# Two output projections of a hybrid transformer on one core: a place of its own for the second chunk of a weight sum, and evictions and norm weights moved to other units and engines

## The chip, the cores and the metric

The kernel runs on one core of a Trainium2 chip. The metric is the device time in microseconds (us) of one execution. One execution was also taken with the hardware profiler, which records every instruction of TensorE (PE, with its weight loads PEld), VectorE (DVE), ScalarE (ACT), GpSimd (POOL) and SyncE (SP), and the DMA transfers.

## The reference, cut to what matters

A model of two layers on 512 tokens of width 1024, all in float32. Layer 0 is attention followed by a gated feed-forward block, layer 1 is an mLSTM followed by another, and a final norm ends it. The change sits in the second half of the two feed-forward blocks and in the final norm:

```
def swiglu(xn, w_in, w_out):
    gu = xn @ w_in
    return (jax.nn.silu(gu[..., :D_FF]) * gu[..., D_FF:]) @ w_out
...
        h = h + swiglu(rms_norm(h, ffn_norm[i]), ffn_w_in[i], ffn_w_out[i])
    return rms_norm(h, final_norm)
```

D_FF is 2816. The product with w_out (2816 by 1024) is called the output projection here; the first one belongs to layer 0, the last one to layer 1. The final norm divides each token's 1024 values by the root of their mean square and multiplies by final_norm, the norm weights.

## The kernel before, in words

**Precision.** Each float32 operand is split into a high part (ACT copies it, rounded) and a low part (DVE subtracts the high part from the original). A product is three matrix products: high by high, low by high, high by low. For a weight chunk the two instructions are lines 209 (ACT) and 210 (DVE) in split_chunk, on 128x1024 values; for an operand of the output projection they are line 1114 (ACT) and the DVE subtraction that is recorded at line 1108.

**The output projection** (output_products, from line 1086). The hidden width is cut into 11 pieces of 256 rows. The first six pieces, paired as three units u = 0, 1, 2, go through a Strassen-like scheme with seven products P1, P2, P5, P6, P7, P3, P4 instead of eight, each made once for every unit; the last five pieces (called rest: 6 to 10) are multiplied plainly, once for each half n of the weight columns. The list items sets the order: P1 three times; P5 and P2 in turn; P6 then P7, in turn with the rest of one half; P3 three times; P4 in turn with the rest of the other half; then the last pieces (tail: 2 in the first projection, 3 in the last). In the last projection the end of that list is P3 u=0, P3 u=1, P3 u=2, P4 u=0, piece 6, P4 u=1, piece 7, P4 u=2, and then pieces 8, 9, 10 as the tail.

work() walks through this list. Ahead of item i it calls prepare for item i+2, which issues the weight loads on SP, the sums of chunks on DVE, and the splits on ACT and DVE. After the last unit of a product it calls the function that then holds for that product: evictions of the accumulators. The tile scheduler puts the instructions of each engine in their final order by dependences and by the order of these calls.

**Places.** Weight chunks of 128x1024 land in a rotating set of three places (tag wraw, line 200); their high and low parts have three places each (whi, wlo). load_chunk (line 198) takes the next wraw place and issues the load on SP at line 201. SP issues its loads in order, so a load that waits for a place holds up those behind it. The tile tag t1 is one place of 128x1024 in the pool of a feed-forward block; in the first half of the block it holds the sums S of Strassen chunks (line 989), and in layer 1 it holds the norm weights gbc afterwards (line 1614).

**P5 in the first projection** (line 1136) needs the sum of two weight chunks. Both are loaded with load_chunk, so each P5 takes two of the three wraw places. DVE adds them at line 1136, subtracts at line 1108 to update the chunk T (places w8), and splits.

**The end of the last projection** (from line 1635). Accumulators are in PSUM banks c11, u_, p5, c22. add_banks (line 1652) adds u_ to the residual tiles ht[tb, 1] on DVE; tb counts the four blocks of 128 tokens, and the second index is the half n of the output columns. output() does, for one accumulator: line 1636, DVE adds it to the residual ht in place; line 1638, ACT squares it and sums the squares into fss; line 1639, GpSimd multiplies ht by the norm weights in place. mean_before (lines 1642 and 1643, DVE) starts the mean. For n = 1 this is done by outputs() after P7 (c22, tb 2 and 3) and after P3 (p5, tb 0 and 1). For n = 0 it is done behind the tail's matmuls, line 1685, tile by tile; the last tile is cut in two halves of 256 columns (finlast is the second). Then lines 1695 to 1700 make the factor r of that block of tokens (DVE, with one square root on ACT), ACT multiplies ht[tb, 1] by r and stores it from its own queue (lines 1702, 1703), and DVE multiplies ht[tb, 0] by r, which SP stores (lines 1704, 1705).

Of the kernel before, what the change touches and what calls it, by code (L numbers as in the profile page):

```python
# [11 lines left out]
F32 = mybir.dt.float32  # L12
F32R = mybir.dt.float32r
I32 = mybir.dt.int32
AF = mybir.ActivationFunctionType
# [56 lines left out]
def tile_hybrid_dilated_attn_mlstm(  # L72
# [1017 lines left out]
    def output_products(layer, fp, wo, sums_of_rows, tail):  # L1090
# [30 lines left out]
        def prepare_product(name, u):  # L1121
            nm = "f%d%s_%dw" % (layer, name, u)
            view = lambda t: t.rearrange("p (k n) -> p k n", k=2)

            def load(hk, n):
                return load_chunk(weight_rows(hk * UNITS + u, n), [P, 2, 512], nm)[0]
            if name == "P1":
                if u % 2 == 0:
                    tw.append(fp.tile([P, 2, 1024], F32, tag="w8", name="f%dT%d" % (layer, u), bufs=2))
                nc.sync.dma_start(view(tw[u // 2][:, u % 2]), weight_rows(u, 0))  # L1130
            t = tw[u // 2][:, u % 2]
            raw = load(*ROWS[name]) if name in ROWS and name != "P1" else t
            if sums_of_rows:

                if name == "P5":
                    nc.vector.tensor_tensor(raw, raw, load(1, 1), op=ALU.add)
                elif name in ("P7", "P3"):
                    subtract(raw, raw, t)
            else:

                if name in ("P5", "P6"):
                    subtract(t, raw, t)
                    raw = t
                elif name == "P7":
                    subtract(raw, t, raw)
                elif name == "P4":
                    subtract(raw, raw, t)
            whl[name, u] = split_chunk((raw, 1024, view, nm))
            if sums_of_rows and name == "P5":
                subtract(t, raw, t)  # L1150

            if name == "P5":
                split_operand(name, u, sums[u])
            elif name == "P6":
                split_operand(name, u, half(u, 1))
            elif name == "P7":
                subtract(sums[u], *((half(u, 1), half(u, 0)) if sums_of_rows else (half(UNITS + u, 1), half(u, 1))))
                split_operand(name, u, sums[u])
            elif name == "P3":
                if not sums_of_rows:  # L1160
                    subtract(half(u, 1), half(UNITS + u, 0), half(u, 1))
                split_operand(name, u, half(UNITS + u, 1) if sums_of_rows else half(u, 1))
            elif name == "P4":
                if sums_of_rows:
                    subtract(half(UNITS + u, 0), half(UNITS + u, 0), half(u, 1))
                split_operand(name, u, half(UNITS + u, 0 if sums_of_rows else 1))
# [51 lines left out]
        def work(product, plain, then):  # L1218

            for i, (kind, *key) in enumerate(items[:-tail]):  # L1220
                prepare(i + AHEAD)
                key = tuple(key)
                if kind == "product":
                    product(*key, ops[key], whl[key])
                    if key[1] == UNITS - 1 and key[0] in then:
                        then[key[0]]()
                else:
                    plain(*key, ops[key[1]], whl[key])
            for i in range(len(items) - tail + AHEAD, len(items)):
                prepare(i)  # L1230
            return [(ops[pi], whl[n, pi]) for _, n, pi in last]
# [3 lines left out]
    with ExitStack() as fctx:  # L1235
        fp = pool(fctx, "ffn0")
        hid, during, prepare, work = output_products(0, fp, ffn_w_out[0], True, 2)
        ffn_in(0, fp, pair, rbc, hook, prepare, hid, during)


        F = [[ps.tile([P, 512], F32, tag=tag, name="fo%d" % n, bufs=3 if tag == "acc" else 2 - (tag == "t"))
              for tag in tags] for n, tags in enumerate((("s", "s", "acc", "acc"), ("o", "o", "acc", "t")))]
        ts = [slice(0, HALF), slice(HALF, SEQ)]
        target = {"P1": (0, 0), "P2": (0, 0), "P5": (0, 1), "P3": (0, 1), "P6": (1, 0), "P7": (1, 0), "P4": (1, 0)}

        def tile_mm(acc, m, b, w, fresh=False):
            for k in range(2):
                for a_, b_ in SPLITS:
                    nc.tensor.matmul(acc, w[a_][:, k, m * P:(m + 1) * P], b[b_][k],  # L1249
                                     start=(fresh and k == 0 and (a_, b_) == SPLITS[0]),  # L1250
                                     stop=(k == 1 and (a_, b_) == SPLITS[-1]), skip_group_check=True)

        def product(name, u, b, w):
            n, t = target[name]
            for m in range(4):
                tile_mm(F[n][m][:, ts[t]], m, b, w, name == "P1" and u == 0)

        def plain(n, pi, b, w):
            for m in range(4):
                tile_mm(F[n][m], m, b, w)  # L1260

        old, h = h, []

        def natural(k, acc):
            t = hp.tile([P, SEQ], F32, tag="h", name="hn%d" % k, bufs=KC + 1)
            nc.vector.tensor_tensor(t.rearrange("p (j c) -> p c j", c=4), acc.rearrange("p (c j) -> p c j", c=4),
                                    old[k].rearrange("p (c j) -> p c j", c=4), op=ALU.add)
            h.append(t)

        def copy_half(t):  # L1270
            for m in range(4):
                nc.scalar.activation(F[1][m][:, ts[t]], F[0][m][:, ts[t]], AF.Copy)

        def add_sum(n):
            for m in range(4):
                o = old[4 * n + m][:, ts[1]]
                nc.vector.tensor_tensor(o, F[1][m][:, ts[0]], o, op=ALU.add)

        def first_tiles():
            for m in range(4):  # L1280
                natural(m, F[0][m])
        last = work(product, plain, {"P1": lambda: copy_half(0), "P5": lambda: copy_half(1),
                                     "P6": lambda: add_sum(0), "P7": lambda: add_sum(1), "P3": first_tiles})
        for m in range(4):
            for b, w in last:
                tile_mm(F[1][m], m, b, w)
            natural(4 + m, F[1][m])
# [298 lines left out]
    with ExitStack() as fctx:  # L1586
# [47 lines left out]
        def output(tb, n, acc, part, cs=slice(0, 512)):  # L1634
            t = ht[tb, n][:, cs]
            nc.vector.tensor_tensor(t, acc[:, cs], t, op=ALU.add)  # L1636
            junk = npl.tile([P, SEQ], F32, tag="sq", name="fsq", bufs=2)
            nc.scalar.activation(junk[:, cs], t, AF.Square, accum_out=fss[:, tb, part:part + 1])  # L1638
            nc.gpsimd.tensor_tensor(t, t, gbc[:, n * 512 + cs.start:n * 512 + cs.stop], op=ALU.mult)

        def mean_before(tb):
            nc.vector.tensor_tensor(fpre[:, tb:tb + 1], fss[:, tb, 0:1], fss[:, tb, 1:2], op=ALU.add)
# [7 lines left out]
        def add_banks(tbs, src):  # L1650
            for m, tb in enumerate(tbs):
                nc.vector.tensor_tensor(ht[tb, 1], src[m], ht[tb, 1], op=ALU.add)
# [13 lines left out]
            for t in range(2):  # L1666
                multiply_half(((c11, u_), (p5, c22))[n][t], a, t, w)

        def after_p7():
            add_banks((2, 3), u_)  # L1670
            outputs((2, 3), c22)
        last = work(product, plain, {"P1": lambda: copy_banks(u_, c11), "P5": lambda: copy_banks(c22, p5),
                                     "P6": lambda: add_banks((0, 1), u_), "P7": after_p7,
                                     "P3": lambda: outputs((0, 1), p5)})

        rest_of = bank("o", "last")
        t = ht[TB - 1, 0][:, 256:]
# [3 lines left out]
        for acc, tb, cs in tiles:  # L1681
# [8 lines left out]
            if cs.stop == 256:  # L1690
                mean_before(tb)
            else:

                v, r, a2 = fv[:, tb:tb + 1], fr[:, tb:tb + 1], fa[:, tb:tb + 1]
                nc.vector.scalar_tensor_tensor(v, fss[:, tb, 2:3], 1.0 / D, fpre[:, tb:tb + 1],  # L1695
                                               op0=ALU.mult, op1=ALU.add)
                nc.scalar.activation(r, v, AF.Sqrt)  # L1697
                nc.vector.reciprocal(r, r)  # L1698
                nc.vector.tensor_scalar(a2, r, v, r, op0=ALU.mult, op1=ALU.mult)  # L1699
                nc.vector.scalar_tensor_tensor(r, a2, -3.0, r, op0=ALU.add, op1=ALU.mult)  # L1700
                t1, t0 = ht[tb, 1], ht[tb, 0]
                nc.scalar.activation(t1, t1, AF.Copy, scale=r)  # L1702
                nc.scalar.dma_start(out[tb * P:(tb + 1) * P, 512:1024], t1)
                nc.vector.tensor_scalar(t0, t0, r, None, op0=ALU.mult)
                nc.sync.dma_start(out[tb * P:(tb + 1) * P, 0:512], t0)


# [22 lines left out]
```

## Time and profile before

| | us |
|---|---|
| median of 3 runs | 1416.81 (1416.67 to 1419.73) |
| the profiled execution | 1416.74 |
| its span, first to last instruction | 1415.0 |
| first projection on PE (line 1249) | 730.9 to 848.4 |
| last projection on PE (lines 1630, 1685) | 1293.6 to 1408.3 |

A row of the timeline gives start, busy time, engine, line, operation and tiles, merged where alike (x2), and in brackets how long the engine was idle before it and whose result ended that. A tile name in the trace leaves out the product's number: f0P_2w_h is the high part of a chunk of unit 2 of some P in the first projection, f1P of the last; f0w and f1w are the rest's chunks, fo and finc, finu, finp, finlast the accumulators. DVE, ACT and PE records overlap a little with the next, because an instruction's record ends after its successor has entered the engine.

### The profile page before, as it was taken

The page shows a single profiled execution, that of the slowest core. Times are in us where ns is not written, and L with a number is a line of the kernel's source. Part 1 is how long each engine was busy: PE and PEld are TensorE (multiplying, and loading weights), DVE is VectorE, ACT ScalarE, POOL GpSimd, SP SyncE. Part 2 cuts the span into 40 slices and gives each one's busy share as a digit, 9 for nine tenths or more (in the row PEclk, how much of TensorE's full clock was granted, in tenths as well). Part 3 has the DMA queues.
Part 4 walks back from the last instruction along what each step waited for, and adds up shares of the span by engine and source line. Part 5 has one row for each costly group of instructions (what it writes and reads, how often), then busy time and mean ns, then how long its engine had stood idle before and what let it go on. Part 6 is the DMA issues. An engine that isn't in the chain of part 4 may idle for free. (4 is left out here: it accounts for less than half of the span.)

```text
span 1415.0 us, 20843 instructions
## 1 busy us (share of the span) xinstructions
PE 1401.2 (99%) x8094; PEld 1235.3 (87%) x8094; DVE 1046.7 (74%) x1798; ACT 634.2 (45%) x1061; POOL 125.3 (9%) x197
## 2 busy tenths in 40 slices
PE   9999999999999999999999999999999999999997
PEld 7888888888888888999998988888888899999876
DVE  7867557566567398877777868998758888778874
ACT  5333224224225244444574343785534344447433
POOL 1011011002003000000000000112101230000011
PEclk9999999999999999999999999999999999999999
DMA  6346235335435434233334433324333562333542
GB/s 196 101 113 205 77 105 177 114 98 141 149 98 130 160 111 143 69 112 120 109 99 136 135 120 92 89 76 117 93 105 104 156 182 80 120 120 107 162 119 104
DMA packets 134650, 171.27 MB, mean 121 GB/s; under 512 B 8276, under 2 KB 110996, under 8 KB 134552
## 3 DMA queue, kind: packets, MB, share of 16 engines
q1 hardware_dynamic: 124848, 140.99, 32.2%
q0 software_dynamic: 8048, 27.84, 7.5%
q8 instruction: 63, 1.03, 0.3%
q10 hardware_dynamic: 1656, 1.12, 0.2%
q14 instruction: 35, 0.29, 0.1%
HBM read 154.19 MB, written 15.73 MB: 120 GB/s over the span
## 5 line engine op out<-in xcount | busy, mean ns | idle before, releaser
L240 PE MATMUL f1j<-n_h,f1j_h 128*128 128x512 f32 x96 | 37.5, 390 | 0.0
L240 PE MATMUL f0j<-n_h,f0j_h 128*128 128x512 f32 x96 | 37.5, 390 | 0.0
L240 PE MATMUL f0j<-n_h,f0j_l 128*128 128x512 f32 x96 | 37.4, 389 | 0.0
L240 PE MATMUL f1j<-n_h,f1j_l 128*128 128x512 f32 x96 | 37.4, 389 | 0.0
L240 PE MATMUL f0j<-n_l,f0j_h 128*128 128x512 f32 x96 | 37.3, 389 | 0.0
L240 PE MATMUL f1j<-n_l,f1j_h 128*128 128x512 f32 x96 | 37.3, 389 | 0.0
L1356 POOL MEMSET gates_h<- 128x1024 f32 x1 | 1.0, 957 | 382.3 <-PE fo L1249 382.3
L1249 PE MATMUL fo<-f0hh,f0w_h 128*128 128x512 f32 x80 | 31.2, 390 | 0.0
L1249 PE MATMUL fo<-f0hl,f0w_h 128*128 128x512 f32 x80 | 31.2, 390 | 0.0
L1249 PE MATMUL fo<-f0hh,f0w_l 128*128 128x512 f32 x80 | 31.1, 389 | 0.0
L1600 POOL DMA_DIRECT2D hD<-hB x32 | 20.6, 650 | 96.6 <-DVE hB L1597 96.0
L539 DVE TENSOR_TENSOR rot<-rot,sinr 32x1024 f32<-32x1024 f32 x24 | 28.9, 1206 | 0.0
L240 PE MATMUL mo<-n_h,mo_k_h 128*128 128x512 f32 x64 | 25.3, 396 | 0.0
L240 PE MATMUL mo<-n_h,mo_k_l 128*128 128x512 f32 x64 | 25.2, 394 | 0.0
L240 PE MATMUL mqk<-n_h,mqk_k_h 128*128 128x512 f32 x64 | 25.1, 392 | 0.0
L240 PE MATMUL mwo<-yo_l,mwo_k_h 128*128 128x512 f32 x64 | 25.1, 392 | 0.0
L240 PE MATMUL mo<-n_l,mo_k_h 128*128 128x512 f32 x64 | 25.1, 392 | 0.0
L240 PE MATMUL mqk<-n_l,mqk_k_h 128*128 128x512 f32 x64 | 25.1, 392 | 0.0
L240 PE MATMUL awo<-ao_h,awo_k_h 128*128 128x512 f32 x64 | 25.1, 392 | 0.0
L240 PE MATMUL mwo<-yo_h,mwo_k_l 128*128 128x512 f32 x64 | 25.0, 391 | 0.0
L240 PE MATMUL mqk<-n_h,mqk_k_l 128*128 128x512 f32 x64 | 25.0, 390 | 0.0
L240 PE MATMUL awo<-ao_h,awo_k_l 128*128 128x512 f32 x64 | 25.0, 390 | 0.0
(2249 smaller groups left out, 5359.4 us busy)
## 6 DMA issues: line engine op xcount, KB each, us to landing
f0j_w<-in_ffn_w_in_dram SPq DMA_DIRECT2D x28, 512.0 KB, 4.0
f1j_w<-in_ffn_w_in_dram SPq DMA_DIRECT2D x28, 512.0 KB, 4.0
f0w_w<-in_ffn_w_out_dram SPq DMA_DIRECT2D x10, 512.0 KB, 3.8
f1w_w<-in_ffn_w_out_dram SPq DMA_DIRECT2D x10, 512.0 KB, 4.4
awo_k_w<-in_attn_w_out_dram SPq DMA_DIRECT2D x8, 512.0 KB, 7.6
mv_k_w<-in_mlstm_w_in_dram SPq DMA_DIRECT2D x8, 512.0 KB, 3.7
mqk_k_w<-in_mlstm_w_in_dram SPq DMA_DIRECT2D x8, 512.0 KB, 3.7
mo_k_w<-in_mlstm_w_in_dram SPq DMA_DIRECT2D x8, 512.0 KB, 3.8
```

What stands on the lines that cost most here:

```text
L240: nc.tensor.matmul(acc, whl[a][:, k, m * P:(m + 1) * P], pairs[b][kk], start=(kk == 0 and (a, b) == SPLITS[0]), stop=(kk == nk - 1 and (a, ...
L539: nc.vector.tensor_tensor(sh, sh, sinr.unsqueeze(1).to_broadcast([R, 2, SEQ]), op=ALU.mult)
L1249: nc.tensor.matmul(acc, w[a_][:, k, m * P:(m + 1) * P], b[b_][k], start=(fresh and k == 0 and (a_, b_) == SPLITS[0]), stop=(k == 1 and (a_ ...
L1356: nc.gpsimd.memset(gh.bitcast(F32), 0.0)
L1600: nc.gpsimd.dma_start(hD[k // 4].rearrange("(b i) x -> i b x", i=R)[:, :, c0:c0 + R], t[R * a_:R * (a_ + 1)])
```

## The change

It has three parts. In the first projection the second chunk of P5's sum is loaded into t1 instead of a wraw place, with a DMA issued directly on SP. In the last projection the evictions of half n = 1 are called after the units (P4, 0) and (P4, 1) instead of after (P7, 2) and (P3, 2); the dictionary's keys become (product, unit) for that, and the other entries keep their place. And the norm weights of half n = 1 are applied by DVE together with r, in one instruction at the end, instead of by GpSimd in output(); ACT then scales and stores half n = 0, and DVE and SP half n = 1.

```
                 if name == "P5":
-                    nc.vector.tensor_tensor(raw, raw, load(1, 1), op=ALU.add)
+                    a22 = fp.tile([P, 1024], F32, tag="t1", name=nm + "2")
+                    nc.sync.dma_start(view(a22), weight_rows(UNITS + u, 1))
+                    nc.vector.tensor_tensor(raw, raw, a22, op=ALU.add)
...
-                    if key[1] == UNITS - 1 and key[0] in then:
-                        then[key[0]]()
+                    if key in then:
+                        then[key]()
...
-            nc.gpsimd.tensor_tensor(t, t, gbc[:, n * 512 + cs.start:n * 512 + cs.stop], op=ALU.mult)
+            if n == 0:
+                nc.gpsimd.tensor_tensor(t, t, gbc[:, cs], op=ALU.mult)
...
-        def after_p7():
-            add_banks((2, 3), u_)
-            outputs((2, 3), c22)
-        last = work(product, plain, {"P1": lambda: copy_banks(u_, c11), "P5": lambda: copy_banks(c22, p5),
-                                     "P6": lambda: add_banks((0, 1), u_), "P7": after_p7,
-                                     "P3": lambda: outputs((0, 1), p5)})
+        last = work(product, plain, {("P1", 2): lambda: copy_banks(u_, c11), ("P5", 2): lambda: copy_banks(c22, p5),
+                                     ("P6", 2): lambda: add_banks((0, 1), u_), ("P7", 2): lambda: add_banks((2, 3), u_),
+                                     ("P4", 0): lambda: outputs((0, 1), p5), ("P4", 1): lambda: outputs((2, 3), c22)})
...
-                nc.scalar.activation(t1, t1, AF.Copy, scale=r)
-                nc.scalar.dma_start(out[tb * P:(tb + 1) * P, 512:1024], t1)
-                nc.vector.tensor_scalar(t0, t0, r, None, op0=ALU.mult)
-                nc.sync.dma_start(out[tb * P:(tb + 1) * P, 0:512], t0)
+                nc.scalar.activation(t0, t0, AF.Copy, scale=r)
+                nc.scalar.dma_start(out[tb * P:(tb + 1) * P, 0:512], t0)
+                nc.vector.scalar_tensor_tensor(t1, t1, r, gbc[:, 512:], op0=ALU.mult, op1=ALU.mult)
+                nc.sync.dma_start(out[tb * P:(tb + 1) * P, 512:1024], t1)
```

More of the change, by code (lines that the diff above doesn't have):

```diff
@@ L1281, in first_tiles @@
                 natural(m, F[0][m])
-        last = work(product, plain, {"P1": lambda: copy_half(0), "P5": lambda: copy_half(1),
-                                     "P6": lambda: add_sum(0), "P7": lambda: add_sum(1), "P3": first_tiles})
+        last = work(product, plain, {("P1", 2): lambda: copy_half(0), ("P5", 2): lambda: copy_half(1),
+                                     ("P6", 2): lambda: add_sum(0), ("P7", 2): lambda: add_sum(1),
+                                     ("P3", 2): first_tiles})
         for m in range(4):
```

## The prediction, made before the result was known

> **What bounds the kernel now.** First the page: the span and the share of the engines.
>
> ```profile
> span 1415.0 us, 20843 instructions
> PE 1401.2 (99%) x8094; PEld 1235.3 (87%) x8094; DVE 1046.7 (74%) x1798; ACT 634.2 (45%) x1061; POOL 125.3 (9%) x197
> ```
>
> TensorE is busy for 99% of the span, so only two things can move the time: stalls of TensorE, and what lies behind its last matmul. The work of TensorE isn't changed. The profiled execution took 1416.74, 1.74 above its span and 0.07 below the median of 1416.81; I sum against 1416.74.
>
> Next, who kept TensorE waiting, asked once for the first output projection (727 to 860) and once for the last one (1290 to 1410). Columns: total, times, longest.
>
> ```profile
> PE fo L1249 <- ACT f0P_2w_h L209: 1.2, 1, 1.2
> PE fo L1249 <- DVE f0P_2w_l L210: 0.4, 1, 0.4
> ...
> PE finu L1630 <- DVE f1P_1w_l L210: 0.6, 1, 0.6
> PE finp L1630 <- DVE f1P L1108: 0.3, 1, 0.3
> PE finp L1630 <- ACT f1P L1114: 0.3, 1, 0.3
> PE finc L1630 <- ACT f1w_h L209: 0.2, 1, 0.2
> ```
>
> These six are all that the change can remove on TensorE. They are larger than their idle time, since a matmul's record is longer than its turn. The timeline of TensorE in both places shows by how much:
>
> ```profile
> 752.61 0.85 PE L1249 MATMUL fo<-f0P,f0P_2w_h 128*128 128x256 f32 x5 [1.17 <-ACT f0P_2w_h L209]
> 753.87 0.39 PE L1249 MATMUL fo<-f0P,f0P_2w_l 128*128 128x256 f32 x1 [0.41 <-DVE f0P_2w_l L210]
> 754.09 0.40 PE L1249 MATMUL fo<-f0P,f0P_2w_h 128*128 128x256 f32 x2
> 754.32 0.40 PE L1249 MATMUL fo<-f0P,f0P_2w_l 128*128 128x256 f32 x2
> 754.56 0.28 PE L1249 MATMUL fo<-f0P,f0P_2w_h 128*128 128x256 f32 x1
> ...
> 1366.70 0.39 PE L1630 MATMUL finp<-f1P_1w_l,f1P 128*128 128x512 f32 x1
> 1366.93 0.39 PE L1630 MATMUL finp<-f1P_1w_h,f1P 128*128 128x512 f32 x1
> 1367.58 0.50 PE L1630 MATMUL finp<-f1P_2w_h,f1P 128*128 128x512 f32 x1 [0.26 <-ACT f1P L1114]
> 1367.92 0.40 PE L1630 MATMUL finp<-f1P_2w_l,f1P 128*128 128x512 f32 x1
> 1368.61 0.73 PE L1630 MATMUL finp<-f1P_2w_h,f1P 128*128 128x512 f32 x2 [0.29 <-DVE f1P L1108]
> ```
>
> A flowing 256-column matmul takes 0.12 from start to start (754.32 to 754.56 for two) of a record of 0.28, so each stall costs 0.16 more than its idle; a 512-column one takes 0.23 of 0.39, again 0.16. The matmul behind a stall starts late as well: 1367.92 is 0.34 after 1367.58, 0.11 too late, and 754.09 is 0.22 after 753.87, 0.10 too late.
> First projection: 1.17 + 0.41 + 2 x 0.16 + 2 x 0.10 = **2.1**. Last one: 0.6 + 0.3 + 0.3 + 0.2 + 4 x 0.16 + 4 x 0.11 = **2.5**. Together 4.6.
>
> **Part 1, the chunk's own place.** Why was P5 u=2 late? VectorE, ScalarE and SP before it:
>
> ```profile
> 736.70 2.54 DVE L210 TENSOR_TENSOR f0P_0w_l<-f0P_0w_w,f0P_0w_h 128x1024 fp32r<-128x1024 f32 x2
> ...
> 741.98 1.23 DVE L1136 TENSOR_TENSOR f0P_1w_w<-f0P_1w_w 128x1024 f32<-128x1024 f32 x1 [2.13 <-DMA f0P_1w_w<-in_ffn_w_out_dram]
> ...
> 750.19 1.23 DVE L1136 TENSOR_TENSOR f0P_2w_w<-f0P_2w_w 128x1024 f32<-128x1024 f32 x1 [2.53 <-DMA f0P_2w_w<-in_ffn_w_out_dram]
> ...
> 751.50 2.01 ACT L209 ACTIVATE f0P_2w_h<-f0P_2w_w 128x1024 fp32r<-128x1024 f32 x2 [2.27 <-DVE f0P_2w_w L1136]
> ...
> 735.07 4.56 SPq L201 DMA_DIRECT2D f0P_1w_w<-in_ffn_w_out_dram  x3
> ...
> f0P_2w_w<-in_ffn_w_out_dram SPq DMA_DIRECT2D x6, 512.0 KB, 4.0
> f1w_w<-in_ffn_w_out_dram SPq DMA_DIRECT2D x10, 512.0 KB, 4.4
> ```
>
> Both sums at L1136 waited for a load, because three places carried four chunks of two steps. Now P5 takes one. In the new order SP issues P5 u=0's second chunk into t1 far ahead, then T, P2 u=0, P5 u=1 (into a wraw place free before 735), P5 u=1's second, P2 u=1, P5 u=2, its second, P2 u=2. t1 is free for u=1 when the sum of u=0 ends; that is where the first of the three issues stands, 735.07. I take 4.4 for a landing throughout: 739.5. VectorE is done with P2 u=0 at 736.70 + 2.54 = 739.2, so the sum of u=1 runs at 739.5 instead of 741.98 and ends at 740.7. Then P5 u=2's second chunk goes out, lands at 745.1, and the sum runs to 746.4 (before: 751.4). Behind it VectorE makes P5's operand (0.7), updates T (1.2) and makes the low part (1.2), while ScalarE makes the high part (1.0, half of 2.01): ready at 749.5. TensorE wants it at 752.61 - 1.33 = 751.3. Margin 1.8: the whole 2.1 goes. What is late next? P2 u=2: its high part needs the place of P5 u=1's, which TensorE leaves one product (24 x 0.12 = 2.9) before 751.3, at 748.4; with 1.0 + 1.2 it is ready at 750.6, wanted at 751.3 + 2.9 = 754.2. Each u has as many loads as before. The added wait is on SP: behind a t1 load stand P2, the next P5 and the rest's chunks; P2 u=1 waits for a wraw place until 737.9 anyway (the first of the two low parts at 736.70), P2 u=2 for the low part of P5 u=1, at 743.8, later than the 740.7 of the t1 load. So I take 2.1, with 0 as the other end (two landings of over 5.3 each would use up the margin).
>
> **Part 2, the evictions.** VectorE and GpSimd where the last projection stalls:
>
> ```profile
> 1362.68 1.27 DVE L1636 TENSOR_TENSOR ht<-finc,ht 128x512 f32<-128x512 f32 x2
> ...
> 1365.01 1.25 DVE L1642 TENSOR_TENSOR fpre<-fss 128x1 f32<-128x1 f32 x1
> 1366.18 0.68 DVE L1108 TENSOR_TENSOR f1hid<-f1hid,f1hid 128x512 f32<-128x512 f32 x1
> ...
> 1367.56 0.99 DVE L1108 TENSOR_TENSOR f1P<-f1hid,f1P 128x512 fp32r<-128x512 f32 x1 [0.63 <-ACT f1P L1114]
> ...
> 1376.20 2.15 DVE L1108 TENSOR_TENSOR f1P_1w_w<-f1P_1w_w,f1T 128x1024 f32<-128x1024 f32 x1
> ...
> 1375.18 0.63 ACT L1638 ACTIVATE fsq<-ht 128x512 f32<-128x512 f32 x1 [2.70 <-DVE fpre L1643]
> ...
> 1364.31 3.69 POOL L1639 TENSOR_TENSOR ht<-ht,gbc 128x512 f32<-128x512 f32 x2 [75.73 <-ACT fsq L1638]
> ...
> 1407.37 0.15 DVE L1642 TENSOR_TENSOR fpre<-fss 128x1 f32<-128x1 f32 x1
> ```
>
> The difference at 1366.18 makes P3 u=2's operand, and it stood behind two evictions (1.27) and a one-column sum that took 1.25 beside a GpSimd multiply where the same line takes 0.15 at 1407.37. The 2.15 at 1376.20 (alike ones take 1.22 to 1.23) is of the same kind.
>
> The Trainium skill explains this, in SBUF — State Buffer, section "SBUF: two separate sides": a VectorE operation with two SBUF inputs and a GpSimd operation lock a shared port pair against each other for a whole instruction. The trace agrees, 1.25 against 0.15.
>
> Now the evictions come after P4 u=0 was queued, and the four GpSimd multiplies of n = 1 are gone. VectorE in the new order: the two sums with u_ end at 1362.7, then the difference, 1363.4; P3 u=2's high part on ScalarE (0.6), 1364.0, and VectorE's low part of the weights (1.2), 1364.6, then of the operand, 1365.3. TensorE wants it at 1366.93 + 0.23 = 1367.16; margin 1.9. Then P4 u=0's chunk sum, 1366.5, its high part, 1367.5, an operand and one eviction on VectorE, 1367.9, low part 1369.1; wanted 12 x 0.23 = 2.7 after 1367.16, at 1369.9, high parts first. Piece 6: split by 1370.3, wanted at 1372.6. P4 u=1: 1374.0, wanted at 1378.1 (24 matmuls later). All six waits fall away, 2.5 here. Next to be late is P4 u=0, with 0.8. The other evictions (0.64 each) and sums stand behind it, ahead of piece 7, which has 3.8 to spare (rival e). I take 2.5, with 1.2 as the other end, if P4 u=0 and P4 u=1 still stall as the 0.2 and 0.6 did.
>
> **Part 3, the norm weights.** What lies behind the last matmul:
>
> ```profile
> 1406.97 0.49 DVE L1704 TENSOR_SCALAR ht<-ht,fr 128x512 f32<-128x512 f32 x1
> ...
> 1408.33 0.42 DVE L1636 TENSOR_TENSOR ht<-finlast,ht 128x256 f32<-128x256 f32 x1 [0.62 <-PE finlast L1685]
> ...
> 1410.54 0.49 DVE L1704 TENSOR_SCALAR ht<-ht,fr 128x512 f32<-128x512 f32 x1
> ...
> 1411.21 0.34 ACTq L1703 DMA_DIRECT2D out_dram<-ht  x1
> ...
> 1407.36 0.77 POOL L1639 TENSOR_TENSOR ht<-ht,gbc 128x256 f32<-128x256 f32 x1 [0.51 <-ACT fsq L1638]
> ...
> 1409.38 0.72 POOL L1639 TENSOR_TENSOR ht<-ht,gbc 128x256 f32<-128x256 f32 x1 [1.25 <-ACT fsq L1638]
> ...
> L228 DVE SCALAR_TENSOR_TENSOR n_l<-hn,cols,n_h x16: 722/744/752, 821.3 to 1069.0; 128x512 fp32r<-128x512 f32 x16
> ```
>
> L1704 becomes an operation with a second tensor. Its nearest row, L228, takes 0.74, so 0.25 more: it ends at 1411.28 instead of 1411.03 and SP's store starts 0.07 after ScalarE's (1411.21) instead of 0.18 ahead. Cost between 0 (ScalarE's store stays last) and 0.25; I take 0.2, as both stores share the DMA engines. ScalarE's scaling now needs GpSimd's last multiply, done at 1410.10, before r at 1410.44: nothing, hidden by 0.3. For the three earlier tiles the extra 0.25 lies in VectorE's idle time.
>
> **Sum:** 1416.74 - 2.1 - 2.5 + 0.2 = **1412.3**.
>
> **Rivals.**
> (a) A lock at the end. L1705 of tile 2 holds VectorE from 1406.97 to 1407.71 and may hold off GpSimd's multiply (1407.36), which then runs to 1408.4; the one-column sum L1646 behind L1705 waits for it, as at 1365.01, and the last eviction comes at 1408.8 instead of 1408.33: 0.5 more, 1412.8. Against it: at 1407.37 that sum slipped in ahead. The Trainium skill (SBUF — State Buffer, "SBUF: two separate sides") speaks for it, since the new operation has two SBUF inputs and locks the pair for its whole length: 1412.8 by that rule.
> (b) Only the first projection gains: evictions at P4 stall TensorE as much as before. 1416.74 - 2.1 + 0.2 = 1414.8. Against: the margins above.
> (c) Only the last gains: t1's loads land late or SP holds P2 back. 1416.74 - 2.5 + 0.2 = 1414.4.
> (d) It doesn't do what it says, both stalls only move: 1416.9.
> (e) Slower: ScalarE has the squares of tiles 1 to 3 queued behind the high part of piece 7, and on VectorE L1646 waits for the square of tile 1 with the low part of piece 7 and all of P4 u=2 behind it. Piece 7 is issued when P4 u=0 is split, 1369.1, and lands at 1373.5; its high part ends at 1374.5, the square (0.63) at 1375.2; two evictions keep VectorE until 1375.5, then two one-column sums (0.3) and the low part (1.2): 1377.0, wanted 12 matmuls after 1378.1, at 1380.8. A landing over 8.6 stalls TensorE one for one (1369.1 + 8.6 + 1.0 + 0.6 + 0.3 + 1.2 = 1380.8), beyond 13.0 the gain of 4.4 is used up, and at 16 it would be 1419.7. Against it: the row's 4.4.
>
> **How the numbers follow.** Forecast 0.58, (a) 0.12, (b) 0.10, (c) 0.08, (d) 0.07, (e) 0.05. A measurement of this kernel tells about 0.2% (2.8) from no change, so faster means below 1414.0: the forecast and (a), and 0.05 for parts of (b) and (c) that gain a little more, 0.75; same: the rest of (b), (c) and (d), 0.20; slower: (e), 0.05. Range: 1411.2 (stalls of 4.9 with the small late starts, no tail cost, and 0.6 for the spread of runs) to 1415.0, which takes in (a) to (c), 0.88 of the chance; (d) and (e) are left out.
>
> **What would show it.** In the changed profile TensorE's waits in both projections have no row above 0.2. L1138 of units 1 and 2 starts near 739.5 and 745 with waits for DMA under 1, and the first projection ends 2.1 earlier. No L1646 beside GpSimd takes 1.25, and GpSimd does nothing before 1390. L1705 takes 0.74, and from the last matmul to the end of the span it is 0.2 longer. I am wrong if TensorE waits for f0P_2w or f1w parts again, or if VectorE's one-column sum before the last eviction takes over 0.5.

## The result, and the profile after

The changed kernel takes **1412.91 us** (median of 7 runs, 1412.43 to 1413.85) against 1417.11 for the kernel before beside it (7 runs): ratio 0.9968, 95% interval 0.9956 to 0.9979, so it is faster, by 0.3%. That is 4.2 us less; the forecast was a gain of 4.4 and a time of 1412.3. The profiled execution took 1413.13. From its page:

```profile
span 1411.4 us, 20838 instructions
PE 1400.3 (99%) x8094; PEld 1236.4 (88%) x8094; DVE 1044.6 (74%) x1798; ACT 633.8 (45%) x1061; POOL 118.5 (8%) x193
```

The span is 3.6 shorter than before's 1415.0, less than the 4.2 of the medians. To see why, I set the starts of the 8094 matmuls of both traces against each other, in order. The changed kernel is behind by 1.0 from the first transposes of the input on (in its profiled run they came that much later; in the other profiled runs they came 0.3 to 1.0 later than before's, too), it is ahead by 1.2 after the first projection, the same 1.2 up to the last one, and 3.9 after it. So the first projection gives **2.17**: 2.08 at the two waits of unit 2, and 0.09 at unit 1, whose first low part VectorE had finished only at 745.61 in the old profile, when TensorE came to it. The last one gives **2.66**, and nothing else between them moves by more than 0.05. From the start of the last matmul to the start of the last instruction (called the tail from here on) it is 7.17 instead of 6.90: **0.27** lost. Net 4.56; less the 1.0 at the start, that is the 3.6 of the spans.

The waits of TensorE, asked for 720 to 860 and for 1285 to 1410, have no row at all: all six waits are gone and none came in their place. VectorE and SP ahead of P5's last unit (timelines of the changed kernel; line 1136 is now 1138, and a22's load is line 1137):

```profile
740.13 1.22 DVE L1138 TENSOR_TENSOR f0P_1w_w<-f0P_1w_w,f0P_1w 128x1024 f32<-128x1024 f32 x1
...
747.08 1.23 DVE L1138 TENSOR_TENSOR f0P_2w_w<-f0P_2w_w,f0P_2w 128x1024 f32<-128x1024 f32 x1 [1.11 <-DMA f0P_2w<-in_ffn_w_out_dram]
...
749.96 2.35 DVE L210 TENSOR_TENSOR f0P_2w_l<-f0P_2w_w,f0P_2w_h 128x1024 fp32r<-128x1024 f32 x2
```

```profile
725.78 0.37 SPq L201 DMA_DIRECT2D f0P_1w_w<-in_ffn_w_out_dram  x1
736.04 0.37 SPq L1137 DMA_DIRECT2D f0P_1w<-in_ffn_w_out_dram  x1
...
741.37 0.37 SPq L1137 DMA_DIRECT2D f0P_2w<-in_ffn_w_out_dram  x1
```

```profile
752.16 0.40 PE L1251 MATMUL fo<-f0P,f0P_2w_h 128*128 128x256 f32 x2
752.40 0.28 PE L1251 MATMUL fo<-f0P,f0P_2w_l 128*128 128x256 f32 x1
```

The first chunk of u = 1 now goes out at 725.78 instead of 735.07, because a place is free for it, and the sum of u = 1 waits for no load, only for VectorE's own work ahead of it. The sum of u = 2 still waits 1.11 for its chunk, issued at 741.37, as soon as the sum of u = 1 had left t1. The first of the two low parts at 749.96 is ready after half of 2.35, at 751.1; TensorE begins the unit at 752.16 and reads that part at 752.40. The stall is gone, and at the unit's start there is 1.0 to spare.

The last projection, VectorE in the changed kernel:

```profile
1361.46 0.68 DVE L1108 TENSOR_TENSOR f1hid<-f1hid,f1hid 128x512 f32<-128x512 f32 x1
...
1363.19 0.68 DVE L1108 TENSOR_TENSOR f1P<-f1hid,f1P 128x512 fp32r<-128x512 f32 x1
...
1365.54 0.68 DVE L1639 TENSOR_TENSOR ht<-finc,ht 128x512 f32<-128x512 f32 x1
```

The operand of P3 u = 2 is ready at 1363.9, and TensorE comes to it at 1366; the first eviction (line 1639 now) stands behind it. The tail: VectorE, then GpSimd, then ScalarE with its queue:

```profile
1403.01 0.75 DVE L1705 SCALAR_TENSOR_TENSOR ht<-ht,fr,gbc 128x512 f32<-128x512 f32 x1
1403.68 0.70 DVE L1646 TENSOR_TENSOR fpre<-fss 128x1 f32<-128x1 f32 x1
1404.41 0.15 DVE L1647 TENSOR_SCALAR fpre<-fpre 128x1 f32<-128x1 f32 x1
1404.48 0.41 DVE L1639 TENSOR_TENSOR ht<-finlast,ht 128x256 f32<-128x256 f32 x1
...
1406.60 0.75 DVE L1705 SCALAR_TENSOR_TENSOR ht<-ht,fr,gbc 128x512 f32<-128x512 f32 x1
```

```profile
1403.47 0.89 POOL L1643 TENSOR_TENSOR ht<-ht,gbc 128x256 f32<-128x256 f32 x1 [0.51 <-ACT fsq L1641]
1405.52 0.72 POOL L1643 TENSOR_TENSOR ht<-ht,gbc 128x256 f32<-128x256 f32 x1 [1.16 <-ACT fsq L1641]
```

```profile
1406.66 0.72 ACT L1703 ACTIVATE ht<-ht,fr 128x512 f32<-128x512 f32 x1 [0.79 <-DVE fr L1701]
1407.41 0.34 ACTq L1704 DMA_DIRECT2D out_dram<-ht  x1
```

The operation at 1406.60 ends at 1407.35 (0.75, where before's took 0.49), so its store no longer leaves 0.16 ahead of ScalarE's but beside it (1407.38 and 1407.41). And rival (a)'s lock did happen: the one-column sum at 1403.68 takes 0.70 beside GpSimd's 1403.47 to 1404.36, where it took 0.15 before. It costs next to nothing, because VectorE had been idle for 0.62 ahead of the eviction behind it and no longer is: from the start of the last matmul to that eviction it is 0.35 instead of 0.32.

### The profile page after: what moved, and what is told of

Its sections match the earlier page's. It is cut to its first block, busy times and chain, and to the rows that moved or that the text cites. A ratio compares the mean times of both kernels' runs of the same rounds, so it can differ in the third digit from the quotient of the medians.

```text
span 1411.4 us, 20838 instructions
## 1 busy us (share of the span) xinstructions
PE 1400.3 (99%) x8094; PEld 1236.4 (88%) x8094; DVE 1044.6 (74%) x1798; ACT 633.8 (45%) x1061; POOL 118.5 (8%) x193
```

## The experiments

**Theory.** The first projection's stalls came from the places, the last one's from where the evictions stood in VectorE's queue, and part 3 only lengthens the tail. **Rivals:** the last projection's stalls came from GpSimd's multiplies holding VectorE, so that part 3 and not part 2 removed them; and part 3's lock in the tail (VectorE held while GpSimd multiplies) costs time. Line numbers in these kernels differ by up to 4 from before's.

### One part at a time

**e1_place_only**, before with part 1 alone:

```
+                    a22 = fp.tile([P, 1024], F32, tag="t1", name=nm + "2")
+                    nc.sync.dma_start(view(a22), weight_rows(UNITS + u, 1))
...
```

> Only the first projection's edit: P5's second chunk in t1. If three wraw places for four chunks made P5 u=2 late, TensorE's two waits there (1.2 and 0.4) go, 2.1 us in all, and the three of the last projection stay: 2.1 us (0.15%) faster than before, the tail unchanged. If both projections only gain together (for instance if the time were taken back later), within 0.5 us of before.

**e2_last_only**, the changed kernel with part 1 undone:

```
-                    a22 = fp.tile([P, 1024], F32, tag="t1", name=nm + "2")
-                    nc.sync.dma_start(view(a22), weight_rows(UNITS + u, 1))
-                    nc.vector.tensor_tensor(raw, raw, a22, op=ALU.add)
+                    nc.vector.tensor_tensor(raw, raw, load(1, 1), op=ALU.add)
```

> Only the last projection's edits: the evictions after P4's units, and n = 1's norm weights on VectorE. The waits of the first projection stay (2.1 us), those of the last go: 2.5 us less there and 0.2 us more behind the last matmul, so about 2.3 us (0.16%) faster than before. If the two halves don't add up, clearly more or less than 2.3.

Measured on one chip against 1417.3: e1 1415.75 (ratio 0.9989, 0.998 to 0.9998), e2 1414.82 (0.9983, 0.9975 to 0.9992). The waits of TensorE in the last projection of e1, and in the first of e2:

```profile
PE finu L1632 <- DVE f1P_1w_l L210: 0.7, 1, 0.7
PE finp L1632 <- DVE f1P L1108: 0.3, 1, 0.3
PE finp L1632 <- ACT f1P L1114: 0.3, 1, 0.3
PE finc L1632 <- ACT f1w_h L209: 0.2, 1, 0.2
```

```profile
PE fo L1249 <- ACT f0P_2w_h L209: 1.1, 1, 1.1
PE fo L1249 <- DVE f0P_2w_l L210: 0.4, 1, 0.4
```

Matmul by matmul, e1 gains 2.17 in the first projection, keeps all four waits of the last, and its tail is 6.88; e2 keeps the two waits of the first, gains 2.67 in the last, and its tail is 7.17. The two halves of the change are independent, and by their traces they add up to the whole: 2.17 + 2.67 - 0.27 = 4.57, against 4.56. By the medians e1 is 1.55 faster and e2 2.48, together 4.0. The time that part 1 can save isn't the same in every run: where the first projection is as before, its waits and late starts cost 2.17 in before's trace, and 2.09, 1.80, 1.91 and 1.80 in those of e2, e3, e4 and e8 (the last three kernels follow below).

### Evictions or multiplies?

**e3_evict_only**, before with part 2 alone (the new dictionary; GpSimd keeps all its multiplies):

```
...
+                                     ("P4", 0): lambda: outputs((0, 1), p5), ("P4", 1): lambda: outputs((2, 3), c22)})
```

> Only the move of the evictions behind P4's units; GpSimd still multiplies n = 1. Theory of the place (VectorE was late because evictions stood ahead of P3 u=2's operand): the stalls at P3 u=2 go (1.1 us of 2.5), and those at piece 6 and P4 u=1 too, unless the multiplies, now at the splits of piece 7, cause one there (0 to 0.5): 2.0 to 2.5 us faster, no tail cost. Theory of the lock (VectorE was late because GpSimd's multiplies block it): four multiplies of 1.3 to 1.9 us still run beside the splits, so stalls of 1 us or more stay, only elsewhere: at most 1.5 us faster.

Measured: 1414.45 (0.9983, 0.9974 to 0.9991), 2.66 gained in the last projection, no wait of TensorE there, tail 6.89. GpSimd and VectorE in it:

```profile
1373.80 1.48 POOL L1640 TENSOR_TENSOR ht<-ht,gbc 128x512 f32<-128x512 f32 x1 [84.40 <-ACT fsq L1639]
1376.73 5.77 POOL L1640 TENSOR_TENSOR ht<-ht,gbc 128x512 f32<-128x512 f32 x3 [1.45 <-ACT fsq L1639]
```

```profile
1374.05 1.25 DVE L1643 TENSOR_TENSOR fpre<-fss 128x1 f32<-128x1 f32 x1
...
1376.96 2.15 DVE L210 TENSOR_TENSOR f1w_l<-f1w_w,f1w_h 128x1024 fp32r<-128x1024 f32 x1
1379.03 2.31 DVE L1108 TENSOR_TENSOR f1P_2w_w<-f1P_2w_w,f1T 128x1024 f32<-128x1024 f32 x1
1381.27 1.78 DVE L1108 TENSOR_TENSOR f1P<-f1hid,f1P 128x512 fp32r<-128x512 f32 x1
```

The lock is all there: four VectorE operations are held 0.9 to 1.1 each (alike ones take 0.15, 1.22, 1.22 and 0.68). But they now stand where the weights of P4 u = 2 and piece 7 have that much to spare, and TensorE waits for none of it. So part 2 alone brings the whole gain of the last projection, and the multiplies need not go for it.

**e4_weights_only**, before with part 3 alone (evictions after P7 and P3 as before):

```
-            nc.gpsimd.tensor_tensor(t, t, gbc[:, n * 512 + cs.start:n * 512 + cs.stop], op=ALU.mult)
+            if n == 0:
+                nc.gpsimd.tensor_tensor(t, t, gbc[:, cs], op=ALU.mult)
...
```

> Only the norm weights of n = 1 on VectorE at the end; the evictions stay behind P7 and P3. Theory of the place: two evictions (1.27 us) still stand ahead of P3 u=2's operand, so most of its stall (1.1 us of 2.5) stays: at most 1.2 us faster after 0.2 for the tail. Theory of the lock: the one-column sums take 0.15 instead of 1.25 and the chunk sum 1.22 instead of 2.15, P3 u=2's operand is there 1.4 us earlier than before, and nearly all of the 2.5 us goes: about 2.2 us faster after 0.2 for the tail.

Measured: 1415.46 (0.9987, 0.9979 to 0.9996); 2.35 gained in the last projection, tail 7.18. VectorE:

```profile
1363.56 1.28 DVE L1636 TENSOR_TENSOR ht<-finc,ht 128x512 f32<-128x512 f32 x2
...
1365.88 0.15 DVE L1643 TENSOR_TENSOR fpre<-fss 128x1 f32<-128x1 f32 x1
1365.95 0.68 DVE L1108 TENSOR_TENSOR f1hid<-f1hid,f1hid 128x512 f32<-128x512 f32 x1
```

The two evictions still stand ahead of the operand, and it is in time all the same, because the one-column sum takes 0.15 and not 1.25. My theory allowed part 3 alone at most 1.2; what came is near what the rival had forecast. So neither is the whole: the stalls needed both, the evictions ahead of the operand and the hold by GpSimd, and to take either away is enough, or nearly so (in e4 0.3 of late start stays at the first matmuls of piece 6). Parts 2 and 3 remove the same stalls, 2.66 and 2.35 alone and 2.66 together; they don't add.

**e8_before_one_input** asks whether the slow sum or the lock behind it is the cause. Before, with one line changed:

```
-            nc.vector.tensor_tensor(fpre[:, tb:tb + 1], fss[:, tb, 0:1], fss[:, tb, 1:2], op=ALU.add)
+            nc.vector.tensor_scalar(fpre[:, tb:tb + 1], fss[:, tb, 0:1], fss[:, tb, 1:2], None, op0=ALU.add)
```

> The kernel before, with the one-column sum at L1642 written as an operation with one tensor input and a per-partition scalar (same result). If a lock between GpSimd and two-input VectorE operations is what delayed the operand of P3 u=2, the sum takes about 0.2 instead of 1.25, but the next two-input operation, the difference f1hid at L1108, is then held off in its place until GpSimd's multiplies end: TensorE's stalls in the last projection stay within 0.5 of before, and the kernel is at most 0.5 us faster (about 1416.6). If the slow sum itself was the cause, the operand is 1.0 earlier, the two stalls of P3 u=2 go, and the kernel is 1 us or more faster (under 1416.1).

Measured: 1416.11 against 1417.14 (0.9992, 0.9983 to 1.0001, which takes in no change at all); the trace gains 1.0 in the last projection. (The 0.37 that it gains in the first is not the edit's, which is not used there: it is the spread named above.) VectorE and GpSimd:

```profile
1365.39 0.20 DVE L1642 TENSOR_SCALAR fpre<-fss 128x1 f32<-128x1 f32 x1
1365.51 1.66 DVE L1108 TENSOR_TENSOR f1hid<-f1hid,f1hid 128x512 f32<-128x512 f32 x1
...
1373.54 0.20 DVE L1642 TENSOR_SCALAR fpre<-fss 128x1 f32<-128x1 f32 x1
1373.66 0.68 DVE L1636 TENSOR_TENSOR ht<-finp,ht 128x512 f32<-128x512 f32 x1
```

```profile
1364.70 3.61 POOL L1639 TENSOR_TENSOR ht<-ht,gbc 128x512 f32<-128x512 f32 x2 [75.81 <-ACT fsq L1638]
1372.86 1.91 POOL L1639 TENSOR_TENSOR ht<-ht,gbc 128x512 f32<-128x512 f32 x1 [4.55 <-ACT fsq L1638]
```

Each expectation was half right. At 1365 the hold only moves on: the sum is free (0.20), the next operation with two SBUF inputs is held instead (1.66 for 0.68), and the two waits for P3 u = 2's operand stay (0.2 and 0.3). At 1373 the next operation takes one input from PSUM (finp) and is not held; that saves a whole microsecond, and the wait of 0.6 in P4 u = 1, which stood at the end of that queue, goes. The lock, not the slow sum, is what holds VectorE, and it costs where a two-input operation is next. The Trainium skill (SBUF — State Buffer, "SBUF: two separate sides") limits the lock to operations with two SBUF inputs, and to the modes that use both ports; on the inputs these rows agree, 0.20 and 0.68 against 1.66; the modes are not tested here.

### Is part 3 needed, and does its lock cost anything?

**e5_one_input_sum**, the changed kernel with that same line changed, so that the tail's sum is not held:

> The changed kernel with the one-column sum L1646 as an operation with one tensor and a scalar per partition instead of two tensors. By the lock (two SBUF inputs against GpSimd) it takes 0.15 to 0.3 us everywhere, also the one behind the last L1705, which took 0.70; VectorE is then idle again before the last eviction, and the end comes no earlier, since that sum's wait was hidden. If any VectorE operation beside GpSimd is held up, it still takes 0.7.

Measured: 1412.59 in one run (span 1410.8), tail 7.15. VectorE:

```profile
1403.15 0.21 DVE L1646 TENSOR_SCALAR fpre<-fss 128x1 f32<-128x1 f32 x1
...
1403.92 0.42 DVE L1639 TENSOR_TENSOR ht<-finlast,ht 128x256 f32<-128x256 f32 x1 [0.37 <-PE finlast L1686]
```

The sum takes 0.21 instead of 0.70 and the eviction waits for TensorE again, but the tail shortens by 0.02 only. The lock in the tail is hidden.

**e7_place_evict**, the changed kernel without part 3 (GpSimd multiplies both halves, the last scaling is as before), beside the changed kernel, twice:

```
-            if n == 0:
-                nc.gpsimd.tensor_tensor(t, t, gbc[:, cs], op=ALU.mult)
+            nc.gpsimd.tensor_tensor(t, t, gbc[:, n * 512 + cs.start:n * 512 + cs.stop], op=ALU.mult)
...
```

> The changed kernel without its third part: t1 for P5's second chunk and the evictions behind P4's units, but GpSimd multiplies n = 1 and ScalarE and VectorE scale as before. From the single parts: 2.1 us less in the first projection, 2.7 us less in the last, nothing more behind the last matmul (6.9 us from its start to the end of the span, as before, against 7.2): 4.8 us faster than before and 0.3 us faster than the changed kernel. If the third part were needed, stalls of TensorE return in the last projection and it is slower than the changed kernel.

> The changed kernel itself beside the one without its third part, on the same chip: 0.3 us slower than that, 4.5 us faster than before, if the tail is all that the third part moves.

> The changed kernel without its third part once more (place and evictions; GpSimd keeps the multiplies of n = 1, and the final scaling is as before), beside the changed kernel itself on the same chip. If the third part costs only the longer last operation, this one is 0.28 us faster than the changed kernel, as the tails of 6.88 and 7.16 say; if the third part saves something elsewhere, it is equal or slower.

> The changed kernel on the same chip, to compare with the kernel without its third part: 0.28 us slower than that one, or equal to it if the third part saves something elsewhere.

| series, both on one chip | before | without part 3 | changed |
|---|---|---|---|
| first | 1416.99 | 1412.64 (0.9970, 0.9959 to 0.9981) | 1412.80 (0.9972, 0.9961 to 0.9983) |
| second | 1417.14 | 1412.73 (0.9968, 0.9956 to 0.9981) | 1413.24 (0.9972, 0.9962 to 0.9982) |

Without part 3 it is 0.16 and 0.51 us faster by the medians; the intervals are too wide to tell that apart, but the traces can: the tails are 6.88 and 6.88 without, 7.16 and 7.18 with it, and TensorE waits in neither projection in any of the four. So part 3 loses 0.3 and saves nothing beside part 2, and parts 1 and 2 alone are the best version here, by an amount that the times don't resolve.

### How much room the own place has

**e6_second_twice**, the changed kernel with each second chunk of P5 loaded twice:

```
+                    for _ in range(2):
                         nc.sync.dma_start(view(a22), weight_rows(UNITS + u, 1))
```

> The changed kernel with each second chunk of P5 loaded twice, the same data into t1, so that it lands later by about 1.3 us. In the changed profile P5 u=2's low part is ready at 751.2 and TensorE wants it at 752.2: a margin of 1.0. Two landings in series each 1.3 later use it up: the waits on f0P_2w parts come back, 1 to 2 us in all. If the margin predicted from the rows of before (1.8) and a single landing counts, at most 0.5 us.

Measured: 1422.13, slower than before (1.0035, 1.0022 to 1.0049). My 1 to 2 us were far too few. SP, the waits of TensorE in the first projection, and the windows (stretch, its length, then the busy time of PE, PEld, DVE, ACT, POOL, then the granted clock, the DMA share and GB/s):

```profile
748.11 0.37 SPq L1138 DMA_DIRECT2D f0P_2w<-in_ffn_w_out_dram  x1
750.50 0.37 SPq L201 DMA_DIRECT2D f0P_2w_w<-in_ffn_w_out_dram  x1
752.01 0.37 SPq L1138 DMA_DIRECT2D f0P_2w<-in_ffn_w_out_dram  x1
```

```profile
PE fo L1252 <- ACT f0P_2w_h L209: 3.0, 1, 3.0
PE fo L1252 <- ACT f0P_1w_h L209: 1.9, 1, 1.9
```

```profile
748.00:750.00 2.00, 0.73 (x6) 0.73 (x7) 1.97 (x3) 1.84 (x2) 0.00 (x0) 1.00 0.32 76
750.00:754.00 4.00, 3.97 (x22) 3.76 (x21) 2.21 (x3) 0.17 (x1) 0.00 (x0) 0.57 0.67 225
754.00:757.00 3.00, 2.99 (x26) 2.78 (x24) 0.00 (x0) 0.63 (x1) 0.00 (x0) 1.00 0.87 308
757.00:760.00 3.00, 0.01 (x1) 0.01 (x1) 2.39 (x3) 1.12 (x2) 0.00 (x0) 1.00 0.11 41
760.00:764.00 4.00, 4.00 (x21) 4.00 (x22) 4.00 (x6) 2.57 (x4) 0.00 (x0) 0.57 0.37 108
764.00:770.00 6.00, 6.00 (x52) 6.00 (x52) 5.19 (x8) 3.29 (x5) 0.00 (x0) 1.00 0.58 182
```

The second load into t1 goes out 3.9 after the first, when that one has landed, where I had let the chunk come only 1.3 later; and the loads behind it on SP are late with it. That gives 4.9 of idle time. The first projection loses 8.6 against the changed kernel; the rest is late starts and the clock. After each idle stretch the mean granted clock is 0.57 over 4 us. In closer windows it is 1.00 from 749.27 to 750.35, 0.50 from 750.35 to 753.76, 1.00 again, and 0.50 from 760.59 to 764.00: 3.41 us at half each time, in which 256-column matmuls start 0.21 apart instead of 0.12. Matmul by matmul, the two stalls with their late starts cost 2.15 and 3.26, and the two slow stretches 1.70 and 1.49: together 8.6. So the place theory holds (a second load's delay comes back as stalls), and its price list lacked a term.

## Why the prediction was right, point by point

**What bounds the kernel.** Right, but for two small late starts that no row of the waits shows (0.09 at unit 1 of the first projection, 0.08 at 1371.31): six waits and the tail were all else that moved.

**Part 1, 2.1.** Measured 2.17, 2.08 of it at the two waits that the term counted, and e1 shows that the place does it. Mis-sized inside: the landing of u = 2's chunk. I took 4.4 for every load; from issue (741.37) to the sum (747.08) it was 5.7. It was in flight together with the loads issued at 740.24 and 744.24, which took 5.5 and 4.6, and from 741.0 to 747.2 the DMA engines were 86% busy. The profiled run is 1.0 later there than before's, so the issue came 0.3 earlier than predicted, the sum 1.0 later than the 745.1 predicted, and the margin was 1.0 and not 1.8. That the margin was wide enough for a landing that I had 1.3 too short is partly luck. The sum of u = 1 waited for nothing but VectorE's own queue. The step "two landings of over 5.3 each would use up the margin" is not tested by this run, in which only one was over it; e6 shows what comes when the margin is gone.

**Part 2, 2.5.** Measured 2.66: the stalls that the term counts all went, and it left out small late starts, 0.08 at 1371.31 and some 0.1 in steps of about 0.02 behind the stalls. The order of work was as predicted: P3 u = 2's operand was ready at 1363.9, where 1365.3 less the 1.2 won by then was forecast; P4 u = 0 was in time, and piece 7 far from late. What failed is a step that the sum didn't use: I put the gain down to the evictions going behind the operand and to the multiplies going, as if both were needed. e3 shows that the first does it alone (2.66), and e4 that the second nearly does (2.35).

**Part 3, 0.2.** Measured 0.27: 0.75 instead of 0.49 at the end is 0.26, and 0.02 of the tail is the lock's, as e5 shows. My upper end was 0.25 and I took 0.2, since ScalarE's store might have hidden a part; all of the longer operation came through, though ScalarE's store still leaves last. GpSimd's last multiply, on which ScalarE's scaling now waits, ends at 1406.24 and is hidden, as said: that scaling starts at 1406.66, after r.

**The rivals.** (a) came true in its mechanism and not in its price: the sum was held to 0.70, but the 0.62 of idle time ahead of the last eviction took it, so it cost 0.02 (e5) and not 0.5. The hold ended about where I had put it: 1408.4 in the old profile's time, and 1404.36 in the new one, which is 3.9 ahead there. But I had let the sum and the operation behind it run after the hold, up to 1408.8; the sum's record ends with the multiply, at 1404.38, and the eviction starts 0.1 later. (b), (c) and (d) fall with the two traces of e1 and e2. (e) didn't come up: no wait for piece 7, even in e3, where its low part is held.

**What would show it.** No TensorE row above 0.2: yes. The sums at 739.5 and 745: 740.1 and 747.1, of which 1.0 is the later start of the run; the first is on time by that, the second about 1 late, with a DMA wait of 1.11, over the 1 that I allowed. "No L1646 beside GpSimd takes 1.25": none does, but one took 0.70, the sign that I had named for being wrong (over 0.5). It was a poor sign, since it measured the hold and not what waited for it. GpSimd's multiplies of the end begin at 1393.58, as said.

**The time.** 1412.3 forecast, 1412.91, 1412.80 and 1413.24 measured. For the sum's 4.4 the two traces show 4.56, and the medians 3.9 to 4.2 against before's of the same series. I summed against a profiled execution (1416.74) that had come to its first transposes 0.3 to 1.0 sooner than every later profiled run and had the dearest stall of the five in the first projection, and before's median grew to 1417.11 with more runs. That these, and not the steps, are why the forecast was low by 0.5 to 0.9 fits the traces; no run singles it out.

## What to carry to other kernels

When two edits are aimed at the same stalls, work out each one alone: here either was enough or nearly so, because the stalls needed two things at once, and the one that also lengthens the tail brings nothing beside the other. A VectorE operation held by GpSimd costs something only where its reader has no slack, so moving it to a slack place is worth as much as removing it; and making one operation immune moves the hold to the next two-input operation behind it. A stall of TensorE of 1.9 us and more was dearer here than its idle time, because slow matmuls followed (1.5 to 1.7 us for each).

## What the runs showed of the hardware

**The clock after a short idle.** Idle stretches of 1.89 and 3.00 on TensorE (e6) were each followed by 3.41 us at half clock, while the 1.17 in the kernel before was followed by none. The slow stretches began 1.1 and 0.6 after TensorE had gone back to work (at 749.27 and 759.99), and 10.24 apart, three times their length. The Trainium skill (TensorE: Matmul & The Clock Gate, "What's actually happening") says that the clock falls to half after an idle window of about 3.4 us, and that the windows run freely. The length of the slow stretch agrees with it, and so does the distance of the two; the idle time doesn't, since 1.89 was enough here. Where between 1.17 and 1.89 the bound lies, and whether it depends on the moment, no run here shows.

**Two inputs or one.** Begun while a GpSimd multiply ran, the sum of two columns took 0.70 to 1.25 as an operation with two tensors, and 0.20 to 0.21 with one tensor and a scalar per partition, on the same data. Begun within 0.05 of the multiply's own start, the operation with two tensors was not held: 0.16 at 1375.93 and 0.15 at 1407.37 in the kernel before.
